# Average pooling in 3-D: TensorE in place of SP waits for the last stores and takes their semaphores back

## The chip, the cores and the metric

The kernel runs on one core of a Trainium2 chip. The metric is the device time of one execution in microseconds (us), as a median of several. The *span* of a profile is shorter: from the first to the last instruction that carries a source line of the kernel. The *page* is the printed summary of one profiled execution. A store has *landed* at the last update that the DMA engines make on its semaphore. Each kernel has one trace, of one execution.

## The reference

The input is 8 x 32 x 32 x 32 x 32 in float32 (33.55 MB), the output its mean over windows of 2 x 2 x 2 (4.19 MB):

```python
window = x[:, :, d_s:d_s + 2, h_s:h_s + 2, w_s:w_s + 2]
result[:, :, i, j, k] = np.mean(window, axis=(-3, -2, -1))
```

## The kernel before

SP issues ten loads of 2 or 4 MB into five buffers. VectorE adds pairs three times. SP issues three stores after the loads:

```python
for t, k0, kb in [(0, 0, 16), (1, 0, 14), (1, 14, 2)]:
    nc.sync.dma_start(out=ov[...], in_=obuf[t][...])
```

After the framework has compiled the program, the kernel rewrites its closing part by hand. The framework would wait for everything, hold a barrier of all engines, and then let GpSimd (POOL) set all semaphores to zero. Here the barrier waits for everything but the stores; POOL clears all semaphores but theirs; and the wait for the stores stands after the barrier, on SP alone:

```python
    kept = [u.id for i in stores for u in i.sync_info.on_update]   # 102, 103, 104
    # ... (cut: SP's final drain no longer waits for `kept`; POOL's clears leave `kept` out)
    for n in kept:
        w = waits[n]
        closing.append(mybir.InstEventSemaphore(
            name=nc.get_next_instruction_name(), engine=nc.sync.engine, ins=[], outs=[],
            sync_info=mybir.SyncInfo(
                on_wait=[w],                       # semaphore n >= 32
                on_update=[mybir.SyncUpdate(
                    sync_type="semaphore", id=n, ant_name=w.ant_name,
                    update_mode="sem-sub-imm", update_value=w.wait_value)])))
```

One such instruction is called a wait-and-subtract below. So the other four engines can go on to the runtime's own closing code while the stores are under way.

Of the kernel before, what the change touches and what calls it, by code (L numbers as in the profile page):

```python
# [1 line left out]

# [4 lines left out]

F32 = mybir.dt.float32
KF = 256


@with_exitstack
def pool_rows(
    ctx: ExitStack,
    tc: tile.TileContext,
    x: bass.AP,
    kernel_size: int,
    out: bass.AP,
):
    nc = tc.nc  # L20
    assert kernel_size == 2, "only kernel_size == 2 supported"

    B, C, D, H, W = x.shape
    P = nc.NUM_PARTITIONS
    assert (B * C, D, H, W) == (2 * P, 32, 32, 32)
    add = mybir.AluOpType.add



    xv = x.rearrange("b c d h w -> (b c) (d h w)")  # L30
    ov = out.rearrange("b c d h w -> (b c) (d h w)")




    pool_in = ctx.enter_context(tc.tile_pool(name="pin", bufs=5))
    pool_out = ctx.enter_context(tc.tile_pool(name="pout", bufs=1))
    obuf = [pool_out.tile([P, 16 * KF], F32, name=f"obuf{t}") for t in range(2)]
    dummy = pool_out.tile([P, 1], F32, name="dummy")


    plan = [
        (0, 0, (32,)),
        (0, 32, (32,)),
        (0, 64, (32,)),
        (0, 96, (32,)),
        (1, 0, (32,)),
        (1, 32, (32,)),
        (1, 64, (16, 16)),
        (1, 96, (16, 16)),  # L50
    ]

    def pool_unit(buf, t, k0, kb):

        od = kb // 8
        a = buf.rearrange("p (o dd e) -> p o dd e", o=od, dd=2)
        b = buf[:, :od * 1024]
        nc.vector.tensor_add(  # L58
            out=b.rearrange("p (o e) -> p o e", o=od), in0=a[:, :, 0], in1=a[:, :, 1])
        bv = b.rearrange("p (e ww) -> p e ww", ww=2)  # L60
        c = buf[:, od * 1024:od * 1536]
        nc.vector.tensor_add(out=c, in0=bv[:, :, 0], in1=bv[:, :, 1])  # L62
        cv = c.rearrange("p (j hh k) -> p j hh k", hh=2, k=16)
        o0 = k0 * KF // 8
        nc.vector.tensor_tensor_reduce(  # L65
            out=obuf[t][:, o0:o0 + od * 256].rearrange("p (j k) -> p j k", k=16),
            in0=cv[:, :, 0], in1=cv[:, :, 1],
            scale=0.125, scalar=0.0, op0=add, op1=add, accum_out=dummy[:, :],
        )

    for t, k0, parts in plan:
        tin = pool_in.tile([P, 32 * KF], F32, tag="tin", name="tin")
        views = []
        o = 0
        for kb in parts:
            v = tin[:, o * KF:(o + kb) * KF]
            nc.sync.dma_start(
                out=v, in_=xv[t * P:(t + 1) * P, (k0 + o) * KF:(k0 + o + kb) * KF])
            views.append((v, k0 + o, kb))
            o += kb  # L80
        for v, k, kb in views:
            pool_unit(v, t, k, kb)


    for t, k0, kb in [(0, 0, 16), (1, 0, 14), (1, 14, 2)]:
        nc.sync.dma_start(
            out=ov[t * P:(t + 1) * P, k0 * KF:(k0 + kb) * KF],
            in_=obuf[t][:, k0 * KF:(k0 + kb) * KF],
        )


def kernel(tc: tile.TileContext, x: bass.AP, kernel_size: int, out: bass.AP):
    nc = tc.nc
    pool_rows(tc, x, kernel_size, out)
    tc.close()
    tc.compile()  # L96
    blocks = nc.main_func.blocks



    opening, program = blocks[0].instructions, blocks[tc.starting_block_idx].instructions
    load = next(i for i in program if isinstance(i, mybir.InstDMACopy))
    assert load.engine == nc.sync.engine
    barrier = next(
        n for n, i in enumerate(opening)
        if i.engine == load.engine and isinstance(i, mybir.InstDrain))
    program.remove(load)
    opening.insert(barrier, load)




    closing = blocks[-1].instructions
    stores = [
        i for i in program
        if isinstance(i, mybir.InstDMACopy) and "out_" in i.outs[0].memref]
    kept = [u.id for i in stores for u in i.sync_info.on_update]
    final = next(
        i for i in closing
        if i.engine == nc.sync.engine and isinstance(i, mybir.InstDrain))  # L120
    waits = {w.id: w for w in final.sync_info.on_wait}
    closing[closing.index(final)] = mybir.InstDrain(
        name=final.name, engine=final.engine, ins=[], outs=[], is_reset_sema=False,
        sync_info=mybir.SyncInfo(
            on_wait=[w for n, w in waits.items() if n not in kept], on_update=[]))


    reset = next(
        n for n, i in enumerate(closing)
        if isinstance(i, mybir.InstDrain) and i.is_reset_sema)  # L130
    first, stop = closing[reset].reset_range_start, closing[reset].reset_range_stop
    assert isinstance(closing[reset + 1], mybir.InstISA)
    while len(closing) > reset:
        closing.pop()
    n = first
    while n < stop:
        m = n
        while m < stop and m not in kept:
            m += 1
        if m > n:  # L140
            closing.append(mybir.InstDrain(
                name=nc.get_next_instruction_name(), engine=nc.gpsimd.engine, ins=[], outs=[],
                is_reset_sema=True, reset_range_start=n, reset_range_stop=m))
            nc.gpsimd.sem_clear(range(n, m))
        n = m + 1
    for n in kept:
        w = waits[n]
        closing.append(mybir.InstEventSemaphore(
            name=nc.get_next_instruction_name(), engine=nc.sync.engine, ins=[], outs=[],
            sync_info=mybir.SyncInfo(  # L150
                on_wait=[w],
                on_update=[mybir.SyncUpdate(
                    sync_type="semaphore", id=n, ant_name=w.ant_name,
                    update_mode="sem-sub-imm", update_value=w.wait_value)])))


# [1 line left out]
_INS = ['x', 'kernel_size']  # L158
_OUTS = [((8, 32, 16, 16, 16), 'float32')]

_NUMBERS = {'kernel_size': 2}


# [26 lines left out]
```

## Time and profile before

| | before |
|---|---|
| time, median of 6 (lowest to highest) | 91.93 us (91.76 to 92.09) |
| span | 86.4 us |
| DMA engines busy, share of the span | 99.2% |
| last store lands, from the span's start | 90.60 us |
| last update of a semaphore in the trace | 92.11 us |

The prediction was made with the first three of these six runs (median 91.97 us). This is part 4 of the page, the chain of work that ended last, as shares of the span by engine and then by line.

```profile
DMA 61%; DVE 37%; issue 0%; DVEq 0%
DMA tin<-in_x_dram 61%; DVE tin L58 21%; DVE tin L62 11%; DVE obuf L65 6%; DVE dummy L65 0%; DVEq L96 0%
```

The chain ends at VectorE's part in the framework's barrier (line 96). The last store, which lands over four microseconds later, isn't in it, nor is anything that waits for it.

The timeline's last line for SP (start, duration, and what) is the issue of the last store, which the prediction takes from it:

```profile
85.23 0.33 SPq L86 DMA_DIRECT2D out_dram<-obuf  x1
```

What follows the landing is read in the trace's record of semaphore updates: when each semaphore was changed, by whatever cause.

### The profile page before, as it was taken

How to read it: one execution, taken by the hardware profiler on the slowest of the kernel's cores; microseconds unless marked ns; L12 is line 12 of the kernel's file. 1: busy time of each engine (PE TensorE's matmuls, PEld its weight loads, DVE VectorE, ACT ScalarE, POOL GpSimd, SP SyncE). 2: the span in 40 equal slices, each digit the busy share in tenths (PEclk: the TensorE clock that was granted, in tenths of full speed). 3: DMA queues.
4: the chain of work that ended last, by engine and by line, in shares of the span. 5: the costliest groups of instructions: out<-in, count | busy, mean ns of one | idle time of the engine just before them, and what ended most of it. 6: DMA issues, size and time to landing. Idle time of an engine off the chain costs nothing.

```text
span 86.4 us, 90 instructions
## 1 busy us (share of the span) xinstructions
DVE 64.0 (74%) x40; POOL 0.2 (0%) x4
## 2 busy tenths in 40 slices
DVE  0000039993999749993999749992999999999994
POOL 0000000000000000000000000000000000000000
DMA  8979997999979999799979999799999999998999
GB/s 243 425 319 470 486 470 319 425 486 486 455 319 440 486 486 410 319 486 486 470 319 425 486 486 440 304 470 387 455 402 455 395 455 410 440 425 319 448 432 408
DMA packets 1634, 36.37 MB, mean 421 GB/s; under 512 B 176, under 2 KB 176, under 8 KB 176
## 3 DMA queue, kind: packets, MB, share of 16 engines
q1 hardware_dynamic: 1634, 36.37, 99.2%
HBM read 33.55 MB, written 4.19 MB: 437 GB/s over the span
## 4 chain that ended last, share of the span: by engine, by line
DMA 61%; DVE 37%; issue 0%; DVEq 0%
DMA tin<-in_x_dram 61%; DVE tin L58 21%; DVE tin L62 11%; DVE obuf L65 6%; DVE dummy L65 0%; DVEq L96 0%
## 5 line engine op out<-in xcount | busy, mean ns | idle before, releaser
L58 DVE TENSOR_TENSOR tin<-tin 128x4096 f32<-128x4096 f32 (+1 forms) x10 | 35.7, 3569 | 20.6 <-DMA tin<-in_x_dram 20.6
L62 DVE TENSOR_TENSOR tin<-tin 128x2048 f32<-128x2048 f32 (+1 forms) x10 | 18.6, 1864 | 0.3
L65 DVE CUSTOM_DVE_ANT_1 obuf<-tin 128x1024 f32<-128x1024 f32 (+1 forms) x10 | 10.1, 1011 | 0.3
L65 DVE DVE_READ_ACCUMULATOR2_ANT dummy<- 128x1 f32 x10 | 0.8, 82 | 0.0
L171 POOL MEMSET const-bfloat16-1.0<- 128x1 bf16 x1 | 0.1, 102 | 0.0
L171 POOL MEMSET const-uint8-127<- 128x1 uint8 x1 | 0.1, 101 | 0.0
L171 POOL MEMSET const-float32-1.0<- 128x1 f32 x1 | 0.1, 99 | 0.0
L171 POOL MEMSET const-float32-0.0<- 128x1 f32 x1 | 0.1, 98 | 0.2 <-issue 0.2
## 6 DMA issues: line engine op xcount, KB each, us to landing
tin<-in_x_dram SPq DMA_DIRECT2D x6, 4096.0 KB, 34.9
tin<-in_x_dram SPq DMA_DIRECT2D x4, 2048.0 KB, 38.0
out_dram<-obuf SPq DMA_DIRECT2D x1, 2048.0 KB, 36.4
out_dram<-obuf SPq DMA_DIRECT2D x1, 1792.0 KB, 9.1
out_dram<-obuf SPq DMA_DIRECT2D x1, 256.0 KB, 5.4
```

The lines of the kernel that those rows point to most:

```text
L58: nc.vector.tensor_add(out=b.rearrange("p (o e) -> p o e", o=od), in0=a[:, :, 0], in1=a[:, :, 1])
L62: nc.vector.tensor_add(out=c, in0=bv[:, :, 0], in1=bv[:, :, 1])
L65: nc.vector.tensor_tensor_reduce(out=obuf[t][:, o0:o0 + od * 256].rearrange("p (j k) -> p j k", k=16), in0=cv[:, :, 0], in1=cv[:, :, 1], s ...
L171: nc = _bacc.Bacc("TRN2", target_bir_lowering=False, num_devices=1)
```

## The change

Its intent is to have another engine than SP, which issues all transfers, do the waiting at the end.

```diff
     kept = [u.id for i in stores for u in i.sync_info.on_update]
+    kept = [n for j, n in enumerate(kept) if n not in kept[j + 1:]]
...
         closing.append(mybir.InstEventSemaphore(
-            name=nc.get_next_instruction_name(), engine=nc.sync.engine, ins=[], outs=[],
+            name=nc.get_next_instruction_name(), engine=nc.tensor.engine, ins=[], outs=[],
```

The first line drops repeated numbers. There are none.

## The prediction

> **What bounds the kernel now.** I read the page first. The heading and part 1 give the span and the only busy engine, part 2 the filling of the DMA engines, part 3 the queue.
>
> ```profile
> span 86.4 us, 90 instructions
> DVE 64.0 (74%) x40; POOL 0.2 (0%) x4
> DMA  8979997999979999799979999799999999998999
> q1 hardware_dynamic: 1634, 36.37, 99.2%
> HBM read 33.55 MB, written 4.19 MB: 437 GB/s over the span
> ```
>
> The 16 DMA engines are full (99.2%) from start to end; VectorE, with 64.0 us, waits 20.6 us for loads. So up to the last instruction the kernel is bound by its 33.55 + 4.19 MB. But the change touches nothing up to there. It touches what lies between the span (86.4 us) and the measured time (91.97 us): 5.6 us, 6% of the time. So I went on to the stores, in the view of DMA issues, and to a table of stretches that runs past the span's end.
>
> ```profile
> out_dram<-obuf SPq DMA_DIRECT2D x1, 1792.0 KB, 9.1
> out_dram<-obuf SPq DMA_DIRECT2D x1, 256.0 KB, 5.4
> ...
> 84.00:86.40 2.40, 1.17 (x3) 0.00 (x0) 1.00 1.00 427
> 86.40:92.00 5.60, 0.00 (x0) 0.00 (x0) 1.00 0.58 241
> ```
>
> The first number after a store's size is microseconds from issue to landing. The timeline has the last store issued at 85.23 us; it lands 5.4 us later, near 90.6. In the last line every engine's busy time is zero and the DMA engines are still 58% busy: the end is a wait for data. The waiting instructions themselves have no source line and are in no view of the page; nor do they count in the span. What is seen around them is the tile framework's last barrier, in the view of line 96:
>
> ```profile
> L96 POOLq EVENT_SEMAPHORE  x2: 17/17/17, 85.9 to 86.0; - x2
> L96 SPq EVENT_SEMAPHORE  x1: 17/17/17, 86.0 to 86.0; - x1
> L96 ACTq EVENT_SEMAPHORE  x1: 17/17/17, 86.0 to 86.0; - x1
> L96 DVEq EVENT_SEMAPHORE  x1: 21/21/21, 86.0 to 86.0; - x1
> L96 PEldq EVENT_SEMAPHORE  x1: 51/51/51, 86.0 to 86.0; - x1
> ```
>
> All five engines pass it at 86.0 us. It doesn't wait for the stores. The same kind of instruction takes 17 ns on SP and 51 ns on TensorE; that will be a term.
>
> The rest comes from the trace's record of semaphore updates, which no view prints. Times are from the span's start:
>
> ```
> sem 97 (framework barrier): 86.000 POOL releases; 86.035 SP, 86.045 ACT, 86.058 DVE, 86.092 PE
> sem 104 (last store): last DMA update 90.603; SP's subtraction 90.637
> sem 2, first closing barrier: 86.315 86.349 86.913 86.957 | 90.765 | 90.809 90.847 90.881 90.928
> clearing: 207-255 from 90.882, 156-206 from 90.945, 54-104 from 90.985, 105-155 from 90.989,
>           3-53: 7 at 91.186, 53 at 91.531 (the others are done by 91.279)
> sem 2, second closing barrier: 91.755 91.790 91.828 91.871 | 91.895 | 91.992 92.030 92.065 92.111
> ```
>
> This is the runtime's postamble. Semaphore 2 is counted up by one engine after the other and back. In the first barrier four updates come before the stores have landed and five after; so the engine that waits for the stores in the kernel of before, SP, is the fifth, the turning point. The owners of the five cleared ranges tell the rest: 207-255 starts first, 117 ns after the turn, so it is SP's. The third update, 86.913, comes late, after the range clears that POOL alone has (they end at 86.37), so POOL is third. The range 3-53 starts last and is cleared slowest (7.5 ns a semaphore against 1.9 for 207-255); with five ranges in engine order it is the first engine's, and the first, by elimination and by its slow sequencer, is TensorE. So I read the order as PE, ACT, POOL, DVE, SP and back to PE. That PE is first rather than second is my inference, not something a label says.
>
> **What the Trainium skill says.** "Runtime: NRT & Kernel Launch", section "The ~15µs preamble/postamble breakdown", lists after the kernel a sync barrier, a reset of 51 semaphores per engine and another barrier, and calls the barrier a serpentine across five engines, some 355 ns in 8 hops of 44. The trace agrees: the undisturbed second barrier takes 92.111 - 91.755 = 356 ns over 8 gaps, and ranges such as 156-206 have 51 numbers. It doesn't name the order of engines. The section "Semaphores 0–2 are reserved" gives 2 to the sync barrier; the trace agrees. "Perfetto Trace Analysis", section "Sequencer-only Instruction (DRAIN, etc)", says that the profile shows such an instruction's execution alone, neither its wait nor the propagation; indeed SP's 4.5 us of waiting at the end appears nowhere as a duration.
>
> **The change part by part.** The line that drops repeated numbers from the list of kept semaphores does nothing here: the three stores use 102, 103 and 104, one each. The instruction streams of both kernels are otherwise equal, but for three wait-and-subtract instructions that move from SP's end to TensorE's. No transfer, VectorE instruction or framework barrier moves, so the stores should land at 90.60 us as before, and the span should stay at 86.4.
>
> Before, from landing to the end of the first closing barrier:
> - SP's subtraction: 90.637 - 90.603 = 34 ns
> - from there to SP's barrier update: 90.765 - 90.637 = 128 ns
> - way back over four engines: 90.928 - 90.765 = 163 ns
> - sum 325 ns. The four outward updates were made while the stores were under way, so they were free.
>
> After:
> - TensorE's subtraction. When both were released by the same update of semaphore 97, SP had counted down after 35 ns and TensorE after 92 (86.092 - 86.000). So 92 ns. The waits on 102 and 103 are over earlier: the last landing on 103 is at 90.118, 485 ns before that on 104.
> - from there to TensorE's barrier update: in the kernel of before 86.315 - 86.092 = 223 ns, with nothing that held it. The second barrier starts 224 ns after the last clearing (91.755 - 91.531), so this looks like a fixed cost of TensorE's way to the barrier.
> - the whole serpentine, out and back, since nobody can count before the first has: 356 ns as in the second barrier (the one before the kernel, from -0.373 to -0.002, took 371).
> - sum 92 + 223 + 356 = 671 ns.
>
> Difference: 671 - 325 = +346 ns. Of this, 58 is the slower subtraction, 95 the slower exit, and 193 the outward half that is no longer hidden. After the barrier all is as before: TensorE is the last to clear (603 ns from 90.928 to 91.531), then 224 and 356 ns. Nothing of the 346 ns lies beside other work, because TensorE's clearing is the path and it starts when the barrier has come back to it. 91.97 + 0.35 = 92.32 us, 0.4% slower.
>
> **The rivals.**
> First, it could be faster: TensorE has the longest work after the barrier, so one could think that its part should be begun sooner, or that SP is relieved. For it: SP's clearing ends at 90.972, 0.56 us before TensorE's. Against: both barriers need all five engines, and TensorE's clearing can't begin before its own wait is over. If TensorE were the last to be asked, at the turn, and ACT or another the first, the serpentine would cost little more and the loss would be the 58 + 95 ns of the slower sequencer, less than 0.2 us: 92.1 us. That is what remains if my order is wrong. A gain of 2% would need 1.84 us, more than half of all that comes after the landing (92.111 - 90.603 = 1.51 us cannot even give it). I see no way to it.
>
> Second, nothing changes: if the measured time ended with the landing of the data, or before the closing barriers, who waits would be no matter, and 91.97 stays. Against: the last barrier update is 92.11 us after the first instruction, within 0.2 us of the measured time, and landing is 1.4 us short of it. So the postamble seems to be counted, though the start of the measured interval is not in the trace.
>
> Third, much slower: a waiting TensorE sequencer might notice a semaphore late, or might have to fetch the instructions of the postamble only after the wait. For it: its slow control instructions. Against: at 86.000 it had been waiting since its barrier update at 0.894 us, 85 us, and was through 92 ns after release; before that its exit of 223 ns already includes whatever it needs to reach the postamble. I would allow some tenths for it: 92.7. The 93.8 us that make 2% would take another 1.5 us.
>
> **Range and chances.** The centre is 92.32. The three runs of before spread over 0.26 us, mostly from when the data lands, I suppose, and a median of a few runs can be off by 0.15. The serpentine's order can take 0.2 away, a late wake-up add 0.2. So 92.02 to 92.60. All of it is within 2%; I give 0.01 to each side.
>
> **What would show it.** In the changed kernel's update record: the updates of semaphore 2 in the first closing barrier must all nine come after the last landing on 104 (five do now), spaced at 23 to 113 ns; TensorE's subtraction on 104 about 92 ns after the landing rather than 34; the first barrier update some 223 ns after that; 7 to 53 cleared some 0.35 us later relative to the landing. The span must stay at 86.4 and the stores' landing at 5.4 us. If some barrier updates still come at 86.3 to 87.0, TensorE is not first, and my 193 ns are wrong by that part; if the gap from landing to the first update is far over 315 ns, a late wake-up or a fetch is the cause; and if the tail grows by 0.35 us and the time doesn't, the measured time doesn't contain it.

## More of the kernel before

The kernel's opening barrier (line 171) has the sequencers' instructions with their source line, so that the engines can be compared there once more (count, least, median and longest ns, first and last start).

```profile
L171 SPq EVENT_SEMAPHORE  x1: 17/17/17, 0.7 to 0.7; - x1
L171 ACTq EVENT_SEMAPHORE  x1: 17/17/17, 0.7 to 0.7; - x1
L171 DVEq EVENT_SEMAPHORE  x1: 21/21/21, 0.7 to 0.7; - x1
L171 PEldq EVENT_SEMAPHORE  x1: 51/51/51, 0.7 to 0.7; - x1
```

They have the durations of the last barrier, which the prediction shows: TensorE's 51 ns against 17 is no accident of one place.

## The result, and the profile after

| | before | after |
|---|---|---|
| time, median of 6 | 91.93 us | 92.33 us (92.21 to 92.54) |
| ratio | | 1.0047, 95% interval 1.0030 to 1.0064 |
| span | 86.4 us | 86.4 us |

A ratio is the mean time of one kernel's runs over that of the other's of the same rounds, so it isn't quite the ratio of the medians. The kernel became 0.3% to 0.6% slower; by the 2% that counts as a difference it is "same". The lines of the page that answer to those shown in the prediction, from the changed kernel:

```profile
span 86.4 us, 90 instructions
DVE 64.0 (74%) x40; POOL 0.2 (0%) x4
q1 hardware_dynamic: 1638, 36.43, 99.4%
out_dram<-obuf SPq DMA_DIRECT2D x1, 1792.0 KB, 9.0
out_dram<-obuf SPq DMA_DIRECT2D x1, 256.0 KB, 5.3
```

The stretch past the span's end in the table of stretches (length, busy time of VectorE and POOL, granted clock, DMA share, GB/s), and the framework's barrier on SP and TensorE (count, least, median and longest ns, first and last start), also from the changed kernel:

```profile
86.40:92.00 5.60, 0.00 (x0) 0.00 (x0) 1.00 0.57 239
...
L96 SPq EVENT_SEMAPHORE  x1: 17/17/17, 86.1 to 86.1; - x1
L96 PEldq EVENT_SEMAPHORE  x1: 51/51/51, 86.1 to 86.1; - x1
```

Nothing in these views tells the two kernels apart: same span, same transfers, same barrier, and landings 37 ns apart. The 0.4 us came in after the landing. The record of semaphore updates of the changed kernel, in us from the span's start:

```
sem 97 (framework barrier): 86.044 POOL releases; 86.078 SP, 86.136 PE
sem 104 (last store): last DMA update 90.566; TensorE's subtraction 90.657
sem 2, first closing barrier: 90.924 90.958 90.997 91.041 91.064 91.162 91.201 91.235 91.282
clearing by TensorE: 7 at 91.497, 53 at 91.846
sem 2, second closing barrier: 92.070 92.104 92.142 92.187 92.210 92.308 92.347 92.381 92.427
```

In the kernel before, four updates of semaphore 2 had been made by 86.957, while the stores were under way. Now none comes before TensorE is through, and all nine follow. Laid side by side, in ns:

| stretch | before (SP) | after (TensorE) | predicted |
|---|---|---|---|
| landing to subtraction | 34 | 91 | 92 |
| subtraction to the engine's update of semaphore 2 | 128 | 267 | 223 |
| from there to the end of the first closing barrier | 163 | 358 | 356 |
| sum, landing to the barrier's end | 325 | 716 | 671 |
| barrier's end to the last clearing by TensorE | 603 | 564 | 603 |
| last clearing to the end of the second barrier | 580 | 581 | 580 |
| total after the landing | 1508 | 1861 | 1854 |

The trace gives +353 ns after the landing; the runs give +0.43 us (0.0047 of 91.93; interval 0.28 to 0.59). They agree within the noise.

Of the 195 ns more in the third row, the way out accounts for 140 (90.924 to 91.064); before, it was hidden under the stores. The other 55 lie on the way back: the sixth update follows the fifth after 98 ns here, and after 44 in the kernel before. So the prediction's name for this term, "the outward half", fits only 140 of the 195. In the first closing barrier that hop takes 98 or 99 ns in all six traces where an engine other than SP waits last, and 43 or 44 in the four where SP does. That VectorE, fourth on the way out, is by then long ready for the way back would explain it; no run tested that.

### The profile page after: what moved, and what is told of

It reads as the page before. It is cut to its first block, busy times and chain, and to the rows that moved or that the text cites. A ratio compares the mean times of both kernels' runs of the same rounds, so it can differ in the third digit from the quotient of the medians.

```text
span 86.4 us, 90 instructions
## 1 busy us (share of the span) xinstructions
DVE 64.0 (74%) x40; POOL 0.2 (0%) x4
## 4 chain that ended last, share of the span: by engine, by line
DMA 61%; DVE 37%; issue 0%; DVEq 0%
DMA tin<-in_x_dram 61%; DVE tin L58 21%; DVE tin L62 11%; DVE obuf L65 6%; DVE dummy L65 0%; DVEq L96 0%
## 5 line engine op out<-in xcount | busy, mean ns | idle before, releaser
L62 DVE TENSOR_TENSOR tin<-tin 128x2048 f32<-128x2048 f32 (+1 forms) x10 | 18.6, 1864 | 0.3
```

Source lines behind the costliest of these rows:

```text
L62: nc.vector.tensor_add(out=c, in0=bv[:, :, 0], in1=bv[:, :, 1])
```

## The experiments

The diffs are against the changed kernel. The theory, A: the cost of waiting last depends on the engine's place in the runtime's closing barrier (PE, ACT, POOL, DVE, SP and back) and on the time that this engine takes from landing to its update. Rival B: place means nothing, only TensorE's sequencer is slow. Rival C: any engine but SP loses as TensorE does. The first four runs shared a chip and their runs of the kernel before (median 91.91 us), the last four another chip (92.02 us). Differences of 0.1 us drown in the noise of the times, so the verdicts rest on the traces, and the times are a check. That one trace of a kernel is enough can be seen from what should repeat: the second closing barrier takes 356 to 358 ns in all ten traces, and the way from the last clearing to it 224.

### ScalarE waits

```diff
-            name=nc.get_next_instruction_name(), engine=nc.tensor.engine, ins=[], outs=[],
+            name=nc.get_next_instruction_name(), engine=nc.scalar.engine, ins=[], outs=[],
```

> ScalarE waits for the stores and subtracts. Theory A (place in the serpentine PE, ACT, POOL, DVE, SP plus the engine's own sequencer): the first update of semaphore 2 still comes at 86.3 us (PE is free), the other eight after the landing. Subtraction about 45 ns after the landing, way to the barrier about 130 ns as SP's, then 321 ns from the second barrier's update 2 to 9: about 500 ns from landing to the barrier's end, against 325 (SP) and 716 (PE): +0.17 us on before. Rival B (only TensorE's slow sequencer matters, not the place): the same as before, 325 ns, +0.00. Rival C (any engine but SP loses what TensorE loses): +0.39.

Measured: 92.24 us, ratio 1.0017 (0.9995 to 1.0040). One update of semaphore 2 at 86.271, then the landing at 90.596, then eight updates from 90.774. 45 ns to the subtraction, 133 to the update, 323 to the barrier's end: 501. So ScalarE is second, as A says. B fails: ScalarE's way of 133 ns is about SP's 128, and yet the barrier ends 176 ns later (501 against 325), because three of the four outward hops (106 ns) come after the landing and the turn takes 98 ns in place of 44. C fails as well. The time alone would not settle it: its interval reaches from -0.05 to +0.37 us.

### VectorE waits

```diff
-            name=nc.get_next_instruction_name(), engine=nc.tensor.engine, ins=[], outs=[],
+            name=nc.get_next_instruction_name(), engine=nc.vector.engine, ins=[], outs=[],
```

> VectorE waits for the stores and subtracts. Theory A: three updates of semaphore 2 at 86.3 to 87 us, six after the landing. Subtraction about 58 ns, way to the barrier about 160 ns (SP's 128 times 1.25 as its control instructions take 21 against 17 ns), then 240 ns from update 4 to 9 of the undisturbed barrier: about 460 ns, +0.13 us on before. Rival B: +0.00 to +0.06. Rival C: +0.39.

Measured: 92.08 us, ratio 1.0010 (0.9988 to 1.0033). Three updates before the landing (86.281, 86.315, 86.879), six after. 58 + 188 + 241 = 487 ns. VectorE is fourth. Its way to the barrier was taken too short by 28 ns; the estimate from the ratio of 21 to 17 ns was poor.

### GpSimd waits

```diff
-            name=nc.get_next_instruction_name(), engine=nc.tensor.engine, ins=[], outs=[],
+            name=nc.get_next_instruction_name(), engine=nc.gpsimd.engine, ins=[], outs=[],
```

> GpSimd waits for the stores and subtracts, after its own range clears. Theory A: two updates of semaphore 2 at 86.3 us, seven after the landing. Subtraction about 35 ns, way to the barrier up to 565 ns (in before 86.348 to 86.913, nothing held it then), then 283 ns from update 3 to 9: about 880 ns, +0.55 us on before, so the worst of all, worse than TensorE although it stands later. If the 565 ns are the cost of the range clears and not of the way to the barrier: about 450 ns, +0.12 us. Rival B: +0.00.

Measured: 92.74 us, ratio 1.0077 (1.0054 to 1.0100). Two updates before the landing, seven after. 49 (expected 35) + 566 + 287 = 902 ns, the worst of the five. The 566 ns are GpSimd's way to the barrier and not a cost of its range clears: those had ended at 86.52, and the landing came at 90.872. An engine that stands later than TensorE loses more than TensorE: place and way are two terms, and neither ranks the engines by itself.

### TensorE waits for two stores, SP for the last

```diff
-            name=nc.get_next_instruction_name(), engine=nc.tensor.engine, ins=[], outs=[],
+            name=nc.get_next_instruction_name(), engine=nc.sync.engine if n == kept[-1] else nc.tensor.engine, ins=[], outs=[],
```

> TensorE waits for the first two stores, SP for the last alone. All theories that put the cost on what follows the last landing: TensorE is through about 90 ns after the landing on semaphore 103 (near 90.12), its way of 223 to 267 ns and the outward half of 139 ns end near 90.6, about when SP is through with semaphore 104 and its own 128 ns: 0.00 to +0.05 us on before. Against it: if TensorE's waits cost by being there, +0.2 or more. It also tells whether two more instructions on TensorE move its way to the barrier from 223 to 267 ns and its delay before clearing from 258 to 215 (seen with three).

Measured: 91.99 us, ratio 0.9999 (0.9976 to 1.0022). The second store landed at 90.105, TensorE subtracted at 90.197 and made the first update at 90.420; the outward half was done at 90.536, 113 ns ahead of the last landing at 90.649. From there 34 + 135 + 163 = 332 ns. So TensorE's waits cost nothing measurable by themselves when they end early enough, here 544 ns before the last landing; what follows the last landing counts. The second thing is a small surprise: TensorE's way was 223 ns and not 267, and its delay from the barrier's end to its first recorded clearing 215 and not 258, so after the landing this kernel needs 1477 ns against 1508 before.

### The changed kernel again

No edit.

> The changed kernel once more, on the chip of the next three. Landing to the end of the first closing barrier again near 716 ns (91 subtraction, 267 way to the barrier, 358 serpentine), against 671 predicted; if the way to the barrier is 223 this time, its 44 ns were chance. Delay of TensorE from the barrier to its first recorded clearing again 215 and not 258. Time +0.3 to +0.45 us on before.

Measured: 92.29 us, ratio 1.0035 (1.0013 to 1.0057). 92 + 267 + 359 = 718 ns, and 217 ns before the first recorded clearing: the 44 ns that the prediction missed are no chance. The total after the landing is 1864 ns, 356 more than before.

### TensorE subtracts in eight steps

```diff
-        closing.append(mybir.InstEventSemaphore(
-            name=nc.get_next_instruction_name(), engine=nc.tensor.engine, ins=[], outs=[],
-            sync_info=mybir.SyncInfo(
-                on_wait=[w],
+        parts = [4] * 8 if n == kept[-1] else [w.wait_value]
+        assert sum(parts) == w.wait_value
+        for k, part in enumerate(parts):
+            closing.append(mybir.InstEventSemaphore(
+                name=nc.get_next_instruction_name(), engine=nc.tensor.engine, ins=[], outs=[],
+                sync_info=mybir.SyncInfo(
+                    on_wait=[w] if k == 0 else [],
...
-                    update_mode="sem-sub-imm", update_value=w.wait_value)])))
...
+                        update_mode="sem-sub-imm", update_value=part)])))
```

> TensorE takes semaphore 104 back in eight steps of 4 in place of one of 32. If TensorE's instructions after the landing all lie on the path, each of the seven added ones shows in the time: by the 151 ns between TensorE's counting down of semaphore 97 and its subtraction from 102 in the changed kernel, about 1.0 us more than that kernel, +1.4 on before. Rival: the time is set by something that runs beside TensorE (DMA, clearing by others): much less than 0.5 more. Side question: if the 44 ns go by TensorE's instruction count in fours (0: 223 and 258; 2: 223 and 215; 3: 267 and 215), ten gives 223 and 215.

Measured: 93.45 us, ratio 1.0154 (1.0136 to 1.0172), so +1.42 us. The trace:

```
sem 104: last DMA update 90.628; 90.720 90.870 91.060 91.211 91.362 91.513 91.664 91.815
sem 2, first closing barrier: 92.037 ... 92.395; second: 93.181 ... 93.539
```

Six of the seven added steps took 150 or 151 ns, one 190. After that TensorE's way was 222 ns and its delay before clearing 215. The total after the landing is 2911 ns, 1403 more than before, and the time grew by 1420 (interval 1250 to 1580): within the noise, all that is added on TensorE after the landing goes into the time. The rival, something beside TensorE that sets the end, is out. It also shows that the measured time goes on past TensorE's subtraction. The page knows nothing of it; here is its heading, and the stretch after the span with the window drawn longer:

```profile
span 86.4 us, 90 instructions
...
86.40:94.00 7.60, 0.00 (x0) 0.00 (x0) 1.00 0.43 180
```

A kernel that is 1.4 us slower has the same span and the same instructions counted, and no engine shows as busy.

### SP subtracts in eight steps

The same edit with `nc.sync.engine`.

> SP takes semaphore 104 back in eight steps of 4, in the place it has in the kernel before. By the 86 ns between SP's counting down of 97 and its subtraction from 102 in the kernel before, seven more cost about 0.6 us on before. If SP's instructions are as slow as TensorE's, about 1.0. If SP's end is not on the path, 0.

Measured: 92.27 us, ratio 1.0032 (1.0014 to 1.0051), +0.29 us. A miss in size: the seven steps took 57 to 59 ns each, 409 in all, and not 86 each. The basis was wrong: the 86 ns between SP's passing of the framework barrier and its next subtraction hold more than one subtraction. The trace's total after the landing grew by 405 ns (1913 against 1508), inside the interval of 0.13 to 0.47 us. SP's end is on the path too, but one such instruction costs SP 58 ns and TensorE 151.

### TensorE waits for the first store only

```diff
-            name=nc.get_next_instruction_name(), engine=nc.tensor.engine, ins=[], outs=[],
+            name=nc.get_next_instruction_name(), engine=nc.tensor.engine if n == kept[0] else nc.sync.engine, ins=[], outs=[],
```

> TensorE waits for the first store alone, SP for the other two. Nothing after the last landing is changed: 325 to 332 ns to the barrier's end, time as before. TensorE has one instruction more: way to the barrier 223 ns, and its delay before clearing either 258 (as with none) or 215 (as with two and three); the first closing barrier's first three or four updates come at 86.4 to 87 us.

Measured: 91.94 us, ratio 0.9999 (0.9978 to 1.0019). 34 + 131 + 163 = 328 ns to the barrier's end; TensorE's way 222, its delay before clearing 256.

### All of them, from the last landing on

| kernel (who waits last) | to subtraction | way to barrier | rest of barrier | total to the end, ns | against before | times say, us |
|---|---|---|---|---|---|---|
| before (SP) | 34 | 128 | 163 | 1508 | | |
| split (SP) | 34 | 135 | 163 | 1477 | -31 | -0.01 |
| TensorE first store only (SP) | 34 | 131 | 163 | 1513 | +5 | -0.01 |
| VectorE | 58 | 188 | 241 | 1674 | +166 | +0.09 |
| ScalarE | 45 | 133 | 323 | 1685 | +177 | +0.16 |
| after (TensorE) | 91 | 267 | 358 | 1861 | +353 | +0.43 |
| after, again (TensorE) | 92 | 267 | 359 | 1864 | +356 | +0.32 |
| SP, eight steps | 443 | 124 | 163 | 1913 | +405 | +0.29 |
| GpSimd | 49 | 566 | 287 | 2089 | +581 | +0.71 |
| TensorE, eight steps | 1187 | 222 | 358 | 2911 | +1403 | +1.42 |

The last column is the ratio less one times the median of the kernel before of the same runs. The column before it is against the one trace of the kernel before. For the eight-step kernels the first number holds all steps.

## Why the prediction was right

**The place in the profile.** The prediction said that nothing up to the landing changes and that the loss falls between landing and end. The span stayed at 86.4 us, the last store's landing at 5.3 against 5.4 us after issue. One witness was chosen badly: that SP's wait appears nowhere as a duration tells nothing, since the page leaves those instructions out altogether. TensorE's instruction of line 96 tells it: it had waited for 85 us and is shown with 51 ns.

**The order of the engines.** That TensorE is first was an inference from the order in which the five ranges are cleared. The changed kernel shows it: no update of semaphore 2 before TensorE's. The runs with ScalarE, VectorE and GpSimd leave one, three and two updates ahead of the landing, so the order on the way out is shown; which engine makes which update on the way back is not. That the range 3-53 is TensorE's has a witness too: with two or three wait-and-subtracts on TensorE its first recorded clearing comes 215 to 217 ns after the barrier's end and not 258. The prediction put the late third update down to GpSimd's range clears; the run with GpSimd shows that its way to the barrier is slow without them.

**The three terms.** The subtraction, 92 ns from the framework's barrier, measured 91. The serpentine, 356 from the second barrier, measured 358. The way to the barrier, 223, was mis-sized: it measured 267 in both runs of the changed kernel. The prediction had read it as "a fixed cost of TensorE's way to the barrier", and it isn't fixed, as the next part shows. The first update came 358 ns after the landing in place of 315. The prediction's statement that after the barrier "all is as before" failed by about the same amount the other way: TensorE's last clearing came 564 ns after the barrier's end and not 603. Of the two errors, +45 in the sum to the barrier's end and -39 after it, 6 ns remain, and 1 more from the last stretch, so the net was 353 for a predicted 346. That they cancel was not foreseen. The centre of 92.32 us, against 92.33, is nearer than noise of 0.15 us deserves; that part is luck.

**The 44 ns.** With 0, 1, 2, 3 and 10 wait-and-subtract instructions on TensorE its way was 223, 222, 223, 267 and 222 ns, its delay before clearing 258, 256, 215, 215 and 215; and with 10 one step took 190 in place of 151. All five fit one extra delay of some 40 ns at one fixed place of TensorE's instruction stream, the fifth instruction or so after the framework's barrier: with few added instructions it falls after the closing barrier, with two it hides in the wait inside the barrier, with three it falls on the way there, with ten among the steps. The idea that it recurs every four instructions is not needed: ten instructions show it once. What the delay is was not tested and stays open; a fetch of instructions, the prediction's third rival, isn't excluded for it.

**The rivals.** "Faster" needed TensorE's later work to begin sooner, and it began later. The prediction's words there are wrong, though not its conclusion: the 1.84 us of a 2% gain are more than all of the 1.51 us after the landing, not just "more than half". "Nothing changes" needed the time to end with the landing or ahead of the barriers. The eight steps refute the first. Against the second, a time that ended with the waiting engine's subtraction would have grown by 57 ns in the changed kernel and by 15 with GpSimd, and the intervals start at 0.28 us (0.12 in its repeat) and 0.50. A time that ended with that engine's first update of semaphore 2 would have grown by 196 and 453 ns, which only the repeat allows. That the second closing barrier lies in the time too rests, as before, on its end (92.11 us) being close to the measured 91.93; no run tested it. "Much slower" by a late wake-up: TensorE subtracted 91 ns after a wait of four microseconds, so it woke no later than at the framework's barrier (92 ns), and beyond the 44 ns its way was not longer.

**A better version.** The split kernel needs 31 ns less than the one before in its trace (the 43 ns of the extra delay hidden, less 7 of a longer way on SP and other scatter), but its time ratio of 0.9999 can't show it. No version tried beats the kernel before measurably; with all five engines tried, SP is the right one for the last wait in this kernel.

## What to carry to other kernels

Who waits last for a kernel's stores is a choice with a price, here 0.17 to 0.58 us over SP by the traces (for ScalarE and VectorE the times alone can't show it): here the best is the engine where the runtime's closing barrier turns round, since all the others have then counted already and the turn itself is 54 ns shorter, and the worst is one that must count early or is slow to get there. A wait that ends early enough before the last landing for its engine and the rest of the way out to be done can stand on another engine. When a change concerns what comes after the last store, the span and the engines' busy times are blind to it; look at the semaphore updates between the last landing and the end, and sum them.

## What the Trainium skill lacked or had wrong

- "Runtime: NRT & Kernel Launch", section "The ~15µs preamble/postamble breakdown", gives the serpentine of the barrier before the kernel as some 355 ns, 8 hops of 44. The sum agrees for the barriers after the kernel that nothing held (356 to 359 ns), and is less near for the one just before it (370 to 372 in all ten traces). The hops aren't equal: 34, 38, 45, 23, 98, 39, 34 and 46 ns in the second closing barrier of the changed kernel, and the 98 becomes 43 or 44 when SP comes late. The page doesn't name the order, which the runs show as TensorE, ScalarE, GpSimd, VectorE, SP on the way out, nor that waiting last is therefore the cheapest on SP (325 ns from the landing to the barrier's end, against 487 to 902).
- No page has the way from a kernel's last semaphore instruction to the runtime's barrier, by engine: SP 124 to 135 ns, ScalarE 133, VectorE 188, TensorE 222 to 267, GpSimd 566.
- The section "The ~15µs preamble/postamble breakdown" puts the semaphore reset after the kernel at about 1.5 us. In the kernel before it took 603 ns from the barrier's end to the last clearing, TensorE's range last (the other four were done 351 ns after the barrier's end), and 827 ns to the second barrier's first update.
- "Advanced Engine Details and Errata", section "Clock Domains", gives the sequencers of SP and TensorE the same 1.2 GHz. The same control instruction takes 17 ns on SP and 51 on TensorE, and a series of subtractions goes at 58 ns each on SP and 151 on TensorE, so equal clocks, which the page states and no run here tests, wouldn't mean equal cost. The page doesn't give the cost of such an instruction by engine.
- No page has the single extra delay of about 40 ns in TensorE's stream a few instructions after the framework's barrier (190 against 151 ns in the run with eight steps).
